# State space halves side by side, six shared PSUM banks, a re-measured issue planner and merged score sums in a two-layer hybrid model

## The chip, the cores and the metric

The kernel runs on one core of a Trainium2 chip. The metric is the device time of one launch in microseconds (us), the median of several runs. All engines of the core run their own instruction queues in order: TensorE (PE, with its weight loads, PEld), VectorE (DVE), ScalarE (ACT), GpSimd (POOL), and SyncE (SP), which issues DMAs.

## The reference

528 tokens (16 meta tokens and 512 others) of width 1024 pass two layers. Each layer mixes tokens in three ways at once, joins the three through one output projection, and then runs a gated feed-forward part:

```python
for l in range(2):
    hn = rmsnorm(h, norm1_g[l])
    sq, sk, sv, rq, rk, rv, rg, u = split(hn @ w_in[l])
    sb_o = stick_breaking(norm(sq), norm(sk), sv)        # 6 heads of 64: exp(logsig(z) + sums over later keys)
    ro = norm(retention(rotary(norm(rq)), rotary(norm(rk)), rv)) * silu(rg)   # 6 heads of 64
    so = s5_mixer(u, ...)          # 256 channels: complex diagonal recurrence, gelu, gate
    h = h + concat(sb_o, ro, so) @ w_out[l]
    hn = rmsnorm(h, norm2_g[l])
    h = h + (silu(hn @ w_gate[l]) * (hn @ w_up[l])) @ w_down[l]
```

The stick-breaking weight of a query and a key needs the sum of log(1 - sigmoid) over the later keys. The state space mixer (s5) needs, once per layer, matrices worked out from its small parameters.

## The kernel before, in words

Activations lie transposed, channels on the 128 partitions and tokens along the free axis: h is 8 tiles of 128 x 528. Every large product is made of three matmuls with 1-pass float32 parts, high x high, high x low and low x high, for each 128 x 128 weight block and each half of 264 tokens. `Unit` loads a block of weights into `wr`, ScalarE rounds it to `wh`, and VectorE or GpSimd subtracts for `wl`. `Norm.parts` makes `xh` (ScalarE) and `xl` (VectorE) of a chunk of h, `Norm.square` the squares, and `Norm.finish` the token scale R, with which VectorE multiplies every projection as it evacuates it. In the last layer the feed-forward part runs on 512 tokens, one matmul each.

One projection is 8 chunks x 3 x 2 = 48 matmuls into two PSUM banks named `pj`. Layer 1 has 22 of them in the order of `PROJ`; the first three are held (`HOLD`) until R is there. The mixers run beside the projections as Python generators ("lanes"): three stick-breaking pairs of heads (tiles z, e, sp, av), a retention lane (rtp, kv, sc, ro), a state space lane (`s5_mix`: es, fr, yps, ysm; `s5_glu`: the gate), the state space parameters (`s5_scalars`, `s5_params`: s5w, bb, btmp, gx, gg, ws, wps, bbd, kps, phasors phr, phi, py, st), and the norm of each head (hps). After each few matmuls `tick` lets lanes issue their next piece. A lane waits until the planner's clock reaches the estimated end of its last piece, which `Timed` and `mm` add up from costs written in the code:

```python
    V = Timed(nc.vector, "V", 70, 1.05)
    SC = Timed(nc.scalar, "SC", 180, 0.7)
    G = Timed(nc.gpsimd, "G", 110, 2.1)
...
        t = 2 * max(107.0, 2 * n) if rhs.dtype == F32 else max(107.0, n) + 3
```

PSUM has 8 banks. `free` lends four to stick-breaking scores and two to everything else a lane does; the projections take theirs, and the next projection's, outside this count. The tile framework places the instructions on the engines by the order of issue as priority, moving an instruction ahead where its inputs are there, and adds the waits; a tile's buffer is reused when its last reader is done.

In `sb_group`, the sums over later key tiles are matmuls with the all-ones matrix `ones`, one for each pair of a key tile and an earlier one in the same group, for the high and the low half of `sp`:

```python
        behind = [(j, q0, q1, o0, i) for j, q0, q1, o0 in g for i in place if i > j]
```

The parameters of layer 1 run on VectorE and GpSimd at the start (`engines` is (V, G)), those of layer 2 on GpSimd alone, (G, G), during layer 1's feed-forward part. One step of `outputs` is on VectorE in both: the imaginary half of `gg`. After the mixers, the output projection is added in three parts (`OUT_PARTS`), each when its inputs are ready: in layer 1 stick-breaking, state space, retention; in layer 2 state space, stick-breaking, retention.

Every instruction of a lane has the line of its helper in the profile: L122 is the `Timed` helper's call, L134 the matmul helper's, L140 the transpose's. So rows are told apart by tile names.

Of the kernel before, what the change touches and what calls it, by code (L numbers as in the profile page):

```python
# [8 lines left out]
F32 = mybir.dt.float32  # L9
# [22 lines left out]
BANKS = 2  # L32
# [57 lines left out]
def hybrid_kernel(ctx, tc, A, out, dbg=None):  # L90
# [16 lines left out]
    class Timed:  # L107


        def __init__(self, eng, key, fixed, each):  # L110
            self.eng, self.key, self.fixed, self.each = eng, key, fixed, each

        def __getattr__(self, name):
            f = getattr(self.eng, name)

            def issue(*a, **k):
                o = k.get("out", a[0] if a else None)
                n = 1
                for d in o.shape[1:]:
                    n *= d  # L120
                spend(self.key, self.fixed + self.each * n)
# [52 lines left out]
    def take(what, n):  # L174

        if free[what] < n:
            yield lambda: free[what] >= n
        free[what] -= n

    def banks(n):  # L180
        yield from take("bank", n)

    def freed(n, what="bank"):
        free[what] += n
# [350 lines left out]
    def s5_params(l, engines, scal, par):  # L535
# [74 lines left out]
        def outputs():  # L610
# [6 lines left out]
            for ri in range(2):  # L617
# [85 lines left out]
    def s5_mix(l, u, par, ys):  # L703
# [3 lines left out]
        for hf in range(2):  # L707
            ut = u[hf]
            uc = tt("uc")
            for t in range(4):  # L710
                for j in range(Q):
                    (SC.copy if (t + j) % 2 else V.tensor_copy)(
                        out=n3(uc)[32 * (3 - j):32 * (3 - j) + 32, t, :],
                        in_=ut[32 * t:32 * t + 32, :].rearrange("p (n q) -> p n q", q=Q)[:, :, j])
                yield
            pr, pi = ph[hf]
            fr, fi, y1, y2 = tt("fr"), tt("fi"), tt("y1"), tt("y2")
            for b in range(2):
                yield from banks(2)
# [567 lines left out]
```

## Time and profile before

| | |
|---|---|
| time, median of 3 runs (lowest to highest) | 1372.97 us (1372.7 to 1373.25) |
| time of the profiled execution | 1372.14 us |
| its span, first to last instruction | 1370.1 us |
| mean granted TensorE clock | 0.994 |
| matmul rows busy | 97% of the span |
| VectorE, ScalarE, GpSimd busy | 58%, 43%, 34% |

The span is what the trace covers; the time lies some 2 us above it. Ends of matmul rows are modelled, and rows overlap, so the starts of successive matmuls tell the pace, and the number of matmuls in a stretch tells how full it is. Where a row shows a bracket, it is the idle time of its engine just before it, and what ended it.

### The profile page before, as it was taken

Reading aid. Unit: us, or ns where it says so; the run is one execution under the profiler, and the core shown is the slowest. Engines: PE = TensorE matmul, PEld = TensorE weight load, DVE = VectorE, ACT = ScalarE, POOL = GpSimd, SP = SyncE. Lnnn points to the kernel's source line nnn. Section 1 sums busy time; section 2 is a strip of 40 time slices with the busy share of each in tenths; the row PEclk is TensorE's granted clock in tenths of the full one; section 3 lists DMA queues with packets and bytes.
Section 4 is the critical chain, followed back from the end, with each engine's and each line's share of the span. In section 5 each row is a group of like instructions: output and inputs, shape, how many; then the busy total and the mean of one; then the engine's idle time right before and its main releaser. Section 6 shows DMA issues by size and latency. Waiting matters only on the chain.

```text
span 1370.1 us, 22529 instructions
## 1 busy us (share of the span) xinstructions
PE 1335.6 (97%) x9188; PEld 1220.8 (89%) x9188; DVE 791.4 (58%) x1270; ACT 589.5 (43%) x936; POOL 464.9 (34%) x588
## 2 busy tenths in 40 slices
PE   6989999999899999999999999999999999999998
PEld 5988989989899999999999899998788888888886
DVE  8974657858456445533566874635485544554453
ACT  5447565446242223322355636664354422342231
POOL 5691545222799212200233451433222200220120
PEclk9999999999999999999999999999999999999999
DMA  4211222223221422232232221213232332333223
GB/s 157 70 62 47 84 66 87 78 69 98 95 79 48 123 78 93 93 93 93 78 93 93 71 94 47 92 43 102 62 123 93 92 95 90 99 102 93 92 81 104
DMA packets 38983, 118.26 MB, mean 86 GB/s; under 512 B 4960, under 2 KB 5472, under 8 KB 38880
## 3 DMA queue, kind: packets, MB, share of 16 engines
q1 hardware_dynamic: 38880, 116.82, 26.8%
q8 instruction: 72, 1.18, 0.4%
q14 instruction: 31, 0.25, 0.1%
HBM read 111.46 MB, written 2.10 MB: 83 GB/s over the span
## 4 chain that ended last, share of the span: by engine, by line
PE 82%; DVE 10%; POOL 3%; ACT 1%; issue 1%; DMA 1%; SPq 0%; DVEq 0%; ACTq 0%
PE pj L134 71%; PE z L134 5%; DVE ysm L122 2%; PE hps L134 1%; PE av L134 1%; PE ro L134 1%; DVE wl L122 1%; DVE s5w L122 1%; PE kps L134 1%; PE sc L134 1%; DVE gg L122 1%; DVE st L122 0%; DVE py L122 0%; POOL py L122 0%; DVE sp L122 0%
## 5 line engine op out<-in xcount | busy, mean ns | idle before, releaser
L134 PE MATMUL pj<-xh,wh 128*128 128x264 f32 (+1 forms) x1792 | 454.4, 311 | 16.8 <-ACT wh L122 5.1
L134 PE MATMUL pj<-xh,wl 128*128 128x264 f32 (+1 forms) x1792 | 453.3, 310 | 3.2 <-DVE wl L122 3.2
L134 PE MATMUL pj<-xl,wh 128*128 128x264 f32 (+1 forms) x1792 | 452.6, 310 | 2.6 <-DVE xl L122 2.6
L122 ACT CAST wh<-wr 128x1024 fp32r<-128x1024 f32 (+3 forms) x209 | 205.8, 987 | 418.8 <-PE pj L134 384.6
L134 PEld LDWEIGHTS pj<-xh,wh 128*128 128x128 f32 x1792 | 298.9, 190 | 36.0 <-issue 5.9
L134 PEld LDWEIGHTS pj<-xl,wh 128*128 128x128 f32 x1792 | 299.4, 190 | 20.5 <-DVE xl L122 3.3
L134 PEld LDWEIGHTS pj<-xh,wl 128*128 128x128 f32 x1792 | 298.9, 190 | 20.7 <-DVE wl L122 3.4
L122 DVE TENSOR_TENSOR wl<-wr,wh 128x1024 fp32r<-128x1024 f32 (+3 forms) x166 | 251.8, 1519 | 69.2 <-ACT wh L122 69.2
L134 PE MATMUL pj<-lo,wh 128*128 128x264 f32 (+1 forms) x720 | 193.4, 322 | 1.3 <-DVE lo L122 1.3
L134 PE MATMUL pj<-hi,wh 128*128 128x264 f32 (+1 forms) x720 | 193.2, 323 | 0.4 <-ACT hi L122 0.4
L134 PE MATMUL pj<-hi,wl 128*128 128x264 f32 (+1 forms) x720 | 193.1, 322 | 0.1
L122 POOL TENSOR_TENSOR up<-ga,up 128x528 f32<-128x528 f32 (+1 forms) x44 | 61.9, 1407 | 345.6 <-DVE up L122 345.5
L122 POOL TENSOR_TENSOR wl<-wr,wh 128x1024 fp32r<-128x1024 f32 (+2 forms) x43 | 96.2, 2237 | 159.4 <-ACT wh L122 153.6
L122 DVE TENSOR_TENSOR h<-h,pj 128x264 f32<-128x264 f32 (+1 forms) x144 | 69.1, 510 | 140.4 <-PE pj L134 140.0
L134 PEld LDWEIGHTS pj<-hi,wh 128*128 128x128 f32 x720 | 120.3, 189 | 11.9 <-ACT hi L122 0.7
L134 PEld LDWEIGHTS pj<-lo,wh 128*128 128x128 f32 x720 | 120.0, 188 | 12.1 <-DVE lo L122 1.5
L134 PEld LDWEIGHTS pj<-hi,wl 128*128 128x128 f32 x720 | 120.0, 189 | 11.1 <-DVE wl L122 0.5
L122 POOL TENSOR_TENSOR lo<-ga,hi 128x528 fp32r<-128x528 f32 (+1 forms) x44 | 58.5, 1330 | 158.0 <-ACT hi L122 157.9
L122 DVE TENSOR_TENSOR up<-pj,R 128x264 f32<-128x264 f32 (+1 forms) x66 | 32.1, 514 | 94.2 <-PE pj L134 94.2
L122 DVE TENSOR_TENSOR ga<-si,up 128x528 f32<-128x528 f32 (+1 forms) x44 | 31.7, 720 | 72.7 <-ACT si L122 57.2
L122 ACT ACTIVATE si<-si,bias 128x528 f32<-128x528 f32 (+1 forms) x44 | 32.2, 731 | 93.9 <-DVE si L122 93.9
L122 POOL TENSOR_TENSOR lo<-sp,hi 128x432 fp32r<-128x432 f32 (+2 forms) x36 | 44.4, 1245 | 73.3 <-ACT hi L122 71.7
(221 smaller groups left out, 1533.9 us busy)
## 6 DMA issues: line engine op xcount, KB each, us to landing
wr<-in_w_in_dram SPq DMA_DIRECT2D x45, 512.0 KB, 3.5
wr<-in_w_gate_dram SPq DMA_DIRECT2D x44, 512.0 KB, 3.5
wr<-in_w_up_dram SPq DMA_DIRECT2D x44, 512.0 KB, 3.5
wr<-in_w_down_dram SPq DMA_DIRECT2D x32, 512.0 KB, 3.6
wr<-in_w_out_dram SPq DMA_DIRECT2D x16, 384.0 KB, 3.3
wr<-in_w_down_dram SPq DMA_DIRECT2D x16, 384.0 KB, 3.1
rc<-in_rope_dram SPq DMA_DIRECT2D x12, 264.0 KB, 3.8
rs<-in_rope_dram SPq DMA_DIRECT2D x12, 264.0 KB, 4.0
```

Of the source, the lines that this page charges most:

```text
L122: return f(*a, **k)
L134: nc.tensor.matmul(out, lhsT=lhsT, rhs=rhs, start=start, stop=stop, skip_group_check=more)
```

## The change

It does the following.

- The start loads the first two weight blocks in pieces between the chunks of h, splits them there, and takes the squares one chunk behind. The first two projections run chunk by chunk together (`two_proj`), the third after them. The state space parameters are spawned after `nrm.finish()`, not before the projections.
- `s5_mix` handles one half of the channels, and the lane spawns it twice, the first when the first half of u is there.
- `BANKS` goes from 2 to 6, and the scores take from the same six (at most four).
- `Timed` gets costs for each kind of operation; strided outputs count twice. The matmul's cost changes too.
- In `sb_group` the matmuls with `ones` that read the same operand for two query tiles become one, with an output of two pieces and an operand read twice.
- In `outputs` the sign of the imaginary half goes into `bbd` and into `xi`; the `gg` step becomes an addition on the parameters' engine. The lane then waits 2 us longer, by the planner's clock, before the `kps` matmuls.

```diff
-BANKS = 2
+BANKS = 6
...
-    V = Timed(nc.vector, "V", 70, 1.05)
-    SC = Timed(nc.scalar, "SC", 180, 0.7)
-    G = Timed(nc.gpsimd, "G", 110, 2.1)
+    V = Timed(nc.vector, "V", {"one": (150, 1.05), "two": (160, 1.2), "tensor_scalar": (150, 0.55),
+                               "tensor_tensor_scan": (180, 2.2)})
+    SC = Timed(nc.scalar, "SC", {"one": (230, 0.8), "two": (230, 0.8)})
+    G = Timed(nc.gpsimd, "G", {"one": (180, 2.1), "two": (180, 2.1), "memset": (100, 0.85)})
...
-        n = out.shape[-1] / 2.4
-        t = 2 * max(107.0, 2 * n) if rhs.dtype == F32 else max(107.0, n) + 3
+        n = math.prod(out.shape[1:]) / 2.4
+        t = 2 * max(109.0, 2 * n + 3) if rhs.dtype == F32 else max(110.0, 1.055 * n + 5)
...
-                        if ri:
-                            V.scalar_tensor_tensor(out=o, in0=a, scalar=-1.0, in1=b, op0=ALU.mult, op1=ALU.subtract)
-                        else:
-                            sub(o, a, b)
+                        (add if ri else sub)(o, a, b)
...
-                    engines[ri].tensor_copy(
+                    engines[ri].tensor_scalar(
...
-                        in_=src[64 * q:64 * q + 64])
+                        in0=src[64 * q:64 * q + 64], scalar1=-1.0 if ri else 1.0, scalar2=None, op0=ALU.mult)
+            now[0][1] += 2000
...
-            V.tensor_tensor(out=xi, in0=fr, in1=pi, op=ALU.mult)
+        V.scalar_tensor_tensor(out=xi, in0=fr, scalar=-1.0, in1=pi, op0=ALU.mult, op1=ALU.mult)
...
+        behind = {}
+        for j, q0, q1, o0 in g:
+            for i, (g1, o1, p0) in place.items():
+                if i > j:
+                    a = max(q0, p0)
+                    behind.setdefault(i, (g1, o1 + a - p0, q1 - a, []))[3].append(o0 + a - q0)
...
+        for g1, o1, w, to in behind.values():
+            d, c = zp[:, to[0]:to[0] + w], slice(o1, o1 + w)
+            if len(to) == 2:
+                f = to[1] - to[0]
+                d = zp[:, to[0] + w - f:to[0] + w + f].rearrange("p (t c) -> p t c", t=2)[:, :, f - w:]
             for part in range(2):
-                mm(zp[:, o0 + a - q0:o0 + q1 - q0], lhsT=ones, rhs=hl[g1][part][:, o1 + a - p0:o1 + q1 - p0],
+                x = hl[g1][part][:, c]
+                mm(d, lhsT=ones, rhs=x[:, None, :].to_broadcast([P, 2, w]) if len(to) == 2 else x,
                    start=False, stop=True, more=True)
...
-        freed(1, "scores")
+        freed(1, "scores", "bank")
...
-                yield from take("scores", 2)
+                yield from take(2, "scores", "bank")
...
+    units += [Unit(*plan[0]), Unit(*plan[1])]
+    for k in range(KD):
         nc.sync.dma_start(out=h[k], in_=A["h0"][k])
...
+        if k < 4:
+            q = [(units[k % 2], k // 2, 4)]
+        elif k < 6:
+            q = [(units[k % 2], 1, 2)]
+        for u, i, pieces in q:
+            c = u.load(i, pieces)
+            nrm.parts(k)
+            for _ in u.split(c):
+                pass
...
+        if k:
+            nrm.square(k - 1)
+    nrm.square(KD - 1)
...
-    spawn(first_params())
...
+        def two_proj():
+
+            ws = [weight(), weight()]
+            pss = [open_ps(T), open_ps(T)]
+            xh, xl = nrm.x
+            for k in range(KD):
+                for ps, w in zip(pss, ws):
+                    mm3(ps, tuple(t[:, k:k + 1, :] for t in w), (xh[k:k + 1], xl[k:k + 1]), first=k == 0, last=k == KD - 1)
+            return pss
...
-            yield lambda: ("u", 1) in got and bool(par)
-            ys, so = [], []
-            yield from s5_mix(l, [got["u", 0], got["u", 1]], par[0], ys)
-            yield from s5_glu(l, ys, so)
+            yield lambda: ("u", 0) in got and bool(par)
+            ys, so = {}, []
+            spawn(s5_mix(l, 0, got["u", 0], par[0], ys), now[0][1])
+            yield lambda: ("u", 1) in got
+            spawn(s5_mix(l, 1, got["u", 1], par[0], ys), now[0][1])
+            yield lambda: len(ys) == 2
+            yield from s5_glu(l, [ys[0], ys[1]], so)
...
             if i == HOLD[l]:
                 nrm.finish()
+                if l == 0:
+                    spawn(first_params())
```

## Rows read from the trace of the kernel before

**Rows 1.** The page's first part: busy time, share of the span, instructions.

```profile
PE 1335.6 (97%) x9188; PEld 1220.8 (89%) x9188; DVE 791.4 (58%) x1270; ACT 589.5 (43%) x936; POOL 464.9 (34%) x588
```

**Rows 2.** Stretches: length, then busy us (instructions) of PE, PEld, DVE, ACT, POOL; clock.

```profile
0.00:13.00 13.00, 5.76 (x23) 5.15 (x24) 7.45 (x27) 7.93 (x14) 8.36 (x36) 1.00 0.80 262
13.00:25.00 12.00, 9.43 (x75) 9.00 (x75) 11.93 (x26) 7.87 (x13) 9.52 (x5) 1.00 0.23 78
25.00:37.40 12.40, 8.39 (x55) 7.96 (x53) 11.55 (x47) 3.15 (x5) 3.97 (x6) 0.86 0.25 89
74.00:92.00 18.00, 13.48 (x83) 12.82 (x82) 16.92 (x55) 10.18 (x19) 15.85 (x40) 0.81 0.09 30
279.00:287.00 8.00, 6.30 (x37) 5.63 (x36) 4.95 (x14) 3.26 (x9) 0.59 (x2) 0.79 0.17 49
366.00:375.50 9.50, 5.72 (x36) 5.54 (x35) 6.91 (x10) 2.15 (x3) 9.42 (x14) 0.82 0.13 45
500.00:525.00 25.00, 25.00 (x208) 25.00 (x207) 14.13 (x18) 9.39 (x13) 5.34 (x4) 1.00 0.26 86
```

**Rows 3.** Timeline of TensorE, front: start us, length us, what [idle before <-ended by].

```profile
28.95 0.52 PE L134 MATMUL pj<-xh,wl 128*128 128x264 f32 x2 [3.19 <-DVE wl L122]
...
35.93 0.28 PE L134 MATMUL nps<-hi,meanw 128*128 128x264 f32 x1
...
37.42 0.39 PE L134 MATMUL pj<-xh,wh 128*128 128x264 f32 x1 [0.83 <-ACT R L122]
```

**Rows 4.** Timelines of ScalarE, VectorE and GpSimd, front.

```profile
12.62 1.99 ACT L122 ACTIVATE xh<-h,cols 128x528 fp32r<-128x528 f32 x3
...
12.93 2.38 DVE L122 TENSOR_SCALAR s5w<-s5w 128x16 f32<-128x16 f32 x2
...
19.61 0.76 DVE L122 SCALAR_TENSOR_TENSOR xl<-h,cols,xh 128x528 fp32r<-128x528 f32 x1
...
12.80 2.41 POOL L122 TENSOR_TENSOR wl<-wr,wh 128x1024 fp32r<-128x1024 f32 x1 [1.90 <-ACT wh L122]
```

**Rows 5.** Timeline of TensorE, sums over later key tiles.

```profile
159.85 0.23 PE L134 MATMUL z<-hi,ones 128*128 128x144 f32 x1
...
160.02 0.22 PE L134 MATMUL z<-hi,ones 128*128 128x16 f32 x1
...
160.21 0.36 PE L134 MATMUL z<-hi,ones 128*128 128x256 f32 x1
```

**Rows 6.** Groups of TensorE by shape: count | busy us, mean ns | idle.

```profile
L134 PE MATMUL z<-lo,ones 128*128 128x16 f32 x72 | 17.8, 258 | 0.0
```

**Rows 7.** Timelines of TensorE and VectorE, 77 to 88 us.

```profile
77.44 0.39 PE L134 MATMUL pj<-xh,wh 128*128 128x264 f32 x1 [2.52 <-ACT we L122]
...
87.83 0.39 PE L134 MATMUL pj<-xh,wh 128*128 128x264 f32 x1 [1.16 <-DVE sq L122]
...
79.58 2.34 DVE L122 TENSOR_TENSOR st<-st 128x4 f32<-128x4 f32 x1
```

**Rows 8.** Stretches of tile es alone (PE, PEld, DVE), and TensorE's timeline at 282.

```profile
140.00:170.00 30.00, 2.12 (x16) 2.03 (x16) 2.87 (x8) 1.00 0.30 91
...
200.00:230.00 30.00, 2.13 (x16) 1.97 (x16) 2.86 (x8) 1.00 0.22 68
...
281.96 0.51 PE L134 MATMUL pj<-lo,wh 128*128 128x264 f32 x2 [1.26 <-DVE lo L122]
```

**Rows 9.** Timelines of GpSimd, VectorE and TensorE, 365 to 372 us.

```profile
365.40 2.64 POOL L122 TENSOR_TENSOR gx<-braw,s5p 128x640 f32<-128x640 f32 x2
...
368.07 2.94 DVE L122 SCALAR_TENSOR_TENSOR gg<-gx,gx 64x320 f32<-64x320 f32 x4 [3.96 <-POOL gx L122]
...
371.61 0.56 PE L134 MATMUL pj<-xh,wh 128*128 128x264 f32 x1 [3.78 <-DVE ga L122]
```

**Rows 10.** Waits of TensorE, whole span: us in total, times, longest us.

```profile
PE kps L134 <- POOL bbd L122: 1.5, 1, 1.5
...
PE hps L134 <- ACT hsq L122: 1.3, 1, 1.3
```

More of the change, by code (lines that the diff above doesn't have):

```diff
@@ L107, in hybrid_kernel, with __init__ @@
     class Timed:
-        def __init__(self, eng, key, fixed, each):
-            self.eng, self.key, self.fixed, self.each = eng, key, fixed, each
+        def __init__(self, eng, key, kinds):
+            self.eng, self.key, self.kinds = eng, key, kinds
         def __getattr__(self, name):
@@ L117, in issue @@
                 o = k.get("out", a[0] if a else None)
[L118 to L121, printed above, removed]
+                n = math.prod(o.shape[1:]) * (2 if o.ap[-1][0] > 1 else 1)
+                two = [x for x in (k.get("in0"), k.get("in1")) if x is not None]
+                kind = name if name in self.kinds else "two" if len(two) == 2 and not any(
+                    x.space == PSUM for x in two) else "one"
+                fixed, each = self.kinds[kind]
+                spend(self.key, fixed + each * n)
                 return f(*a, **k)
             return issue
-    V = Timed(nc.vector, "V", 70, 1.05)
-    SC = Timed(nc.scalar, "SC", 180, 0.7)
-    G = Timed(nc.gpsimd, "G", 110, 2.1)
+    V = Timed(nc.vector, "V", {"one": (150, 1.05), "two": (160, 1.2), "tensor_scalar": (150, 0.55),
+                               "tensor_tensor_scan": (180, 2.2)})
+    SC = Timed(nc.scalar, "SC", {"one": (230, 0.8), "two": (230, 0.8)})
+    G = Timed(nc.gpsimd, "G", {"one": (180, 2.1), "two": (180, 2.1), "memset": (100, 0.85)})
     def mm(out, lhsT, rhs, start, stop, more=False):
-        n = out.shape[-1] / 2.4
-        t = 2 * max(107.0, 2 * n) if rhs.dtype == F32 else max(107.0, n) + 3
+        n = math.prod(out.shape[1:]) / 2.4
+        t = 2 * max(109.0, 2 * n + 3) if rhs.dtype == F32 else max(110.0, 1.055 * n + 5)
         spend("PE", t / 2 if 64 in (rhs.shape[0], out.shape[0]) else t)
@@ L172, in hybrid_kernel, with take, freed @@
     free = {"bank": BANKS, "scores": ZBANKS, "group": GROUPS}
[L174 to L178, printed above, removed]
+    def take(n, *what):
+        if any(free[w] < n for w in what):
+            yield lambda: all(free[w] >= n for w in what)
+        for w in what:
+            free[w] -= n
     def banks(n):
-        yield from take("bank", n)
-    def freed(n, what="bank"):
-        free[what] += n
+        yield from take(n, "bank")
+    def freed(n, *what):
+        for w in what or ("bank",):
+            free[w] += n
     def tick(most=TICKS):
@@ L791, in s5_glu @@
+        ys[hf] = y
+        yield
     def s5_glu(l, ys, res):
@@ L881, in sb_pair @@
         sets = ((G_A,), (G_B2, G_B1))
-        yield from take("group", 2)
+        yield from take(2, "group")
         started.append(weights(sets[0]))
@@ L887, in sb_pair @@
             if groups is sets[0]:
-                yield from take("group", 4)
+                yield from take(4, "group")
                 started.append(weights(sets[1]))
@@ L1075, in hybrid_kernel, with proj @@
         mix = [None] * 8
-        def proj(n, p):
-            w = weight()
+        def proj(w):
             ps = open_ps(T)
@@ L1129, in hybrid_kernel @@
         for i, (n, p) in enumerate(proj_order(l)):
-            held.append((n, p, proj(n, p)))
+            if l == 0 and i < 2:
+                if i == 0:
+                    first = two_proj()
+                held.append((n, p, first[i]))
+            else:
+                held.append((n, p, proj(weight())))
             if i == HOLD[l]:
                 nrm.finish()
+                if l == 0:
+                    spawn(first_params())
             if i >= HOLD[l]:
```

191 lines of the change are left out of this document (85 added, 106 removed).

## The prediction

> **What bounds the kernel now.** I read the page's busy times first. The matmul rows cover 97% of the span [rows 1], so time can come off only where TensorE has less to do or stands still; a faster VectorE, ScalarE or GpSimd is worth something only through TensorE. But a busy row is no proof of full speed, so next I cut the span into stretches and counted matmuls. In an undisturbed stretch of the feed-forward part 208 matmuls of 264 columns pass in 25 us, 0.120 us each, at granted clock 1.00, the 2.4 GHz level [rows 2]. Against that yardstick five places stand out.
>
> - Front: 23, 75 and 55 matmuls by 13, 25 and 37.4 us, 153 in all, 18.4 us of work in 37.4 us [rows 2]. 19 us are lost.
> - 74 to 92: 83 where 150 would fit, 8.0 us lost, clock 0.81 [rows 2].
> - 279 to 287: 37 where 67 would fit, 3.6 us, clock 0.79 [rows 2].
> - 366 to 375.5: 36 where 79 would fit, 5.2 us, clock 0.82 [rows 2].
> - Single waits elsewhere, of which two of 1.5 and 1.3 us are shown [rows 10].
>
> A clock below 1.00 is a piece of such a stretch at 1.2 GHz: TensorE had just stood still (3.78 us before 371.61 [rows 9]), and then runs at half speed. So a wait that goes takes a second bill with it, which the counts contain.
>
> Last I read, with the timeline of each engine, what ends these waits. I sum against the profiled execution's own 1372.14 us (span 1370.1); it lies 0.83 us under the median of the runs, 0.06%, and I use one number for both.
>
> **Part 1: the first two blocks side by side (front).** Before, the first projection takes 6 matmuls from each chunk of the hidden state as it arrives, and the second and third follow. After, two weight blocks come in with the chunks and each chunk feeds 12. The DMAs move the same bytes; one more issue stands in SP's queue. When is the last chunk ready? ScalarE has its high half at 14.61 (12.62 + 1.99), but VectorE finishes the low half only at 20.37 [rows 4]: it is in order, and two 16-column scalar operations of the state space part, put in while it was free, took 2.38 us beside GpSimd's 2.41 us subtraction [rows 4]. After, ScalarE carries squares and smaller weight pieces between the chunks, and the scalars are spawned only after the norm's end. They have no input but a small table, so some may still slip in. I take 18.5 for the last low half, between 15.4 (14.61 + one 0.76 operation) and 20.4. By then at least 23 + 5.5 / 0.120 = 69 of the 96 matmuls are done (23 if no more run before 13 us than now), at most the 84 of seven chunks; I take 79. Left are 17 and 48 of the third projection, 65 x 0.120 = 7.8, and the norm's end, 35.93 to 37.42 = 1.5 [rows 3]: 27.8 instead of 37.4. **Gain 10** (9.6). Bounds: 12 if the low half comes at 16.5 (25.8); 3 if it comes at 20.4 with seven chunks done (60 x 0.120 + 1.5 later, 29.1) and the wait of 3.19 us for a weight's low half [rows 3] comes back behind the moved scalars with its half clock, 1.7 (0.14 of 12.4 [rows 2]): 33.9.
>
> **Part 2: issue order by measured durations.** The planner's clock ran ahead of the chip: it took 113 ns for a 264-column matmul that takes 120 [rows 2], and 70 ns as VectorE's fixed cost. So pieces of side work are issued sooner than VectorE can do them, and they clump. From 74 to 92 VectorE is busy 16.92 of 18 us [rows 2], largely with tiny phasor steps, one of which takes 2.34 [rows 7]; the softplus and the evacuations that TensorE needs queue behind, and it waits 2.52 and 1.16 [rows 7]. With costs near the measured ones these steps are spaced. They can go later without harm: the mixer first uses the parameters after 140 [rows 8]. But VectorE's work is not reduced. Of the 8.0 lost I take **4** (0 if the clump only moves, 8 if it dissolves). The single waits go the same way, and the product of the parameters gets 2 us more before its matmuls: of the 1.5 and 1.3 [rows 10] **1.5** (0 to 2.8).
>
> **Part 3: merged sums.** The sums over later key tiles, matmuls with the all-ones matrix, are issued once for two query tiles where the operand is the same. Counted from the code: for each head, pair and layer (12) the high and low halves go from 13 to 8 each, 312 to 192 in all. Of every two 16-wide ones one goes; the trace has 72 of the low half [rows 6], so 36 pairs of halves go. A pair starts 0.19 us before its successor (160.02 to 160.21) [rows 5]: 36 x 0.19 = 6.8. Of the 144-wide 12 pairs go, at 0.17 (159.85 to 160.02) [rows 5], but the merged 288 columns should cost 288/264 of 0.120 = 0.13 each, 0.26 a pair, for 0.34: 12 x 0.08 = 1.0. For the 256-wide, whose merged output has no gap and twice the columns, I take nothing. Sum **8**. TensorE is saturated around these rows, so nothing hides it. Not shown is a matmul whose output lies in two pieces with a gap: 96 of the merged ones write so (the 16s and 144s), and all read the same operand twice. Upper bound 8 (no extra cost); lower 0 (a merged one costs as much as two). I take 8, since in the rows the cost follows the columns above a floor.
>
> No row here shows a gapped write. The Trainium skill's page "PSUM — Partial Sum Buffer" (Specifications) says that any non-contiguous access pattern slows matmuls significantly, without a figure; by it the lower end holds and the whole sum comes to 1352 instead of 1344.
>
> **Part 4: the state space halves side by side.** Now the second half's first products run 60 us after the first's (both 16 matmuls, in 140 to 170 and 200 to 230 [rows 8]), and the gate of this branch ends so late that the output projection over it waits 1.26 us for its low half at 281.96 [rows 8], at the place of the 3.6. Overlapped halves end tens of us earlier. **3** (0 to 3.6). What is late next is the third retention pair, which also needs TensorE there.
>
> **Part 5: the sign moved in the output matrices.** In layer 2's parameters, VectorE's four gg operations wait 3.96 us for GpSimd's gx; the evacuation ga stands behind them in the same queue, and TensorE waits 3.78 for it [rows 9]. The change makes them plain additions on the parameters' engine, here GpSimd, so VectorE no longer waits. GpSimd, busy 9.42 of 9.5 us there [rows 2], gets four operations, each below the 1.3 of a gx [rows 9], up to 5.3 us, behind which the feed-forward's up products wait, and VectorE's last product behind those. **4.5** of 5.2 (0 if that wait takes its place). xi as a three-operand form, and the bbd scaling, stay beside TensorE's work: nothing; without that cover some 0.3 us each.
>
> **Part 6: six shared banks.** Side work may hold six banks at any time, not two plus four for scores. This lets retention and headnorm go on sooner; I count it in the parts above. Against it stand waits of the projections, which take two banks outside the count: the wait at 77.44 is one of a projection for ScalarE's copy out of a wps bank [rows 7]. I charge **3** for new waits of this kind and of the new order (0 to 20).
>
> **Sum.** 10 + 4 + 1.5 + 8 + 3 + 4.5 - 3 = 28: 1372.14 - 28 = **1344 us**.
>
> **Rivals.**
> *Gapped writes cost (0.13).* The merged sums bring nothing: 28 - 8 = 20, 1352. It decides from 81 ns more for each of the 96 (7.8 / 96). For: no such row. Against: only the smooth rows.
> *VectorE takes the front back (0.16).* It is busy 11.93 of 12, 11.55 of 12.4 and 16.92 of 18 us in the stretches from 13 on [rows 2]. If TensorE comes 10 us earlier to evacuations that are no earlier, it waits there. Parts 1 and 2's first term (14) go: 1358. Against: the scalars, phasors and parameters can lie behind.
> *Projections wait for banks (0.08): slower.* With six banks lent out, the next projection needs the two that the last one filled, and waits for VectorE. Some 41 projections run beside side work (22 + 22 - 3). At 28 / 41 = 0.68 us each the gain is gone; at the 1.16 of [rows 7] each it is 48 against 31, 1389. Against: before, 2 + 4 could be lent too, and only waits like 77.44 came of it.
>
> **How the numbers follow.** The forecast has 0.63. All terms at their best give 39.6, 1332, and a little more of the front's 19 makes 1329. Front at 3, gapped writes at full cost, the others at half (2 + 1.4 + 1.5 + 2.2) give some 10 to 12, with rival 2 in view: 1360. Below I leave 0.08, above 0.12. A change within 0.2% (2.7 us) is about what cannot be told from none. Faster 0.91, same 0.02 (where rivals 2 and 3 meet), slower 0.07.
>
> **What would show it.** The fourth projection starts near 28, not 37.4. Ones matmuls number 192, and the 16-wide step from one to the next stays near 0.1 us. The wait of 3.78 for ga and that of 1.26 for the gate's low half are gone; 74 to 92 (now earlier) holds more matmuls at a clock nearer 1.00. The prediction is wrong if the merged rows are spaced twice as far, if projections wait for copies out of other lanes' banks, or if the front's 10 us are lost again before 100.

## The result, and the profile after

The changed kernel takes 1380.97 us, the median of 4 runs (1379.42 to 1382.28); the kernel before took 1373.1 in the same comparison. The ratio is 1.0059, 95% interval 1.0047 to 1.0071: **slower by 0.6%**, where 2% faster was forecast. The profiled execution took 1382.3 us (span 1380.6, mean granted clock 0.986 against 0.994).

The page's busy times answer to [rows 1]; 120 matmuls fewer are recorded, and TensorE's busy time is the same.

```profile
PE 1335.9 (97%) x9068; PEld 1216.3 (88%) x9068; DVE 784.2 (57%) x1261; ACT 587.9 (43%) x937; POOL 470.2 (34%) x598
```

Stretches of the changed kernel, columns as in [rows 2].

```profile
0.00:13.00 13.00, 7.43 (x41) 6.85 (x42) 8.26 (x26) 9.24 (x18) 11.14 (x38) 1.00 0.78 251
13.00:25.00 12.00, 9.27 (x72) 8.63 (x71) 11.57 (x29) 6.23 (x10) 5.62 (x5) 1.00 0.30 107
74.00:92.00 18.00, 13.95 (x92) 13.00 (x94) 17.83 (x79) 5.79 (x12) 15.24 (x44) 0.91 0.17 60
175.00:200.00 25.00, 22.59 (x156) 18.84 (x155) 22.64 (x39) 10.97 (x23) 12.45 (x10) 0.93 0.16 53
279.00:287.00 8.00, 8.00 (x68) 8.00 (x67) 7.28 (x15) 3.62 (x6) 3.95 (x4) 1.00 0.18 51
296.00:306.00 10.00, 8.55 (x40) 7.14 (x41) 1.06 (x3) 4.70 (x9) 1.17 (x1) 0.51 0.08 30
375.00:400.00 25.00, 15.76 (x106) 15.14 (x106) 8.50 (x14) 9.09 (x14) 24.64 (x61) 0.73 0.11 35
500.00:525.00 25.00, 25.00 (x208) 25.00 (x207) 13.26 (x18) 9.48 (x13) 4.19 (x4) 1.00 0.25 86
```

Three of these stretches in the kernel before:

```profile
175.00:200.00 25.00, 24.11 (x194) 22.49 (x190) 15.37 (x37) 15.45 (x32) 9.05 (x6) 1.00 0.20 65
296.00:306.00 10.00, 10.00 (x87) 9.70 (x84) 5.55 (x12) 5.88 (x10) 3.18 (x2) 1.00 0.29 80
375.00:400.00 25.00, 25.00 (x209) 25.00 (x209) 13.36 (x22) 13.52 (x20) 21.54 (x47) 1.00 0.26 85
```

The places that the prediction aimed at are better: 41 matmuls by 13 us instead of 23, 92 instead of 83 from 74 to 92, 68 instead of 37 from 279 to 287 at full clock. But three stretches that were full are not any more: 194 to 156, 87 to 40, 209 to 106 matmuls. At 0.120 us each (an estimate, since not all matmuls are alike) that is some 4.6 + 5.6 + 12.4 = 22.6 us, with TensorE at 1.2 GHz in part of each. The waits behind them (view of waits, TensorE, the largest of 41.0 us in all; 30.8 before):

```profile
PE wps L144 <- POOL ws L125: 9.2, 2, 8.2
PE pj L138 <- ACT wh L125: 5.5, 1, 5.5
PE hps L138 <- ACT hsq L125: 3.6, 3, 1.3
PE pj L138 <- DVE u L125: 3.3, 1, 3.3
PE vps L144 <- DVE sv L125: 2.9, 2, 2.2
PE ro L138 <- DVE sc L125: 2.6, 3, 1.3
PE pj L138 <- DVE wl L125: 2.5, 1, 2.5
PE z L138 <- DVE rk L125: 2.4, 1, 2.4
```

The 3.78 for ga [rows 9] and the 1.26 for the gate's low half [rows 8] are not in the list; wps on ws, over five times as long as either of [rows 10], is new.

By stages, in the profiled executions: layer 1's mixing part (to the first matmul of its feed-forward part) takes 322.8 us instead of 320.6, its feed-forward part (to layer 2's first projection) 405.8 instead of 398.6, and all that follows 1.0 more. So 7.2 of the 10.5 us that the span is longer lie in the feed-forward part that holds the stretch from 375 to 400.

**From 175 to 200 it is VectorE.** Its timeline, then TensorE's row at 182.91:

```profile
169.91 1.78 DVE L125 TENSOR_TENSOR_SCAN fr<-rho,fr 128x132 f32<-128x132 f32 x2
...
176.40 3.39 DVE L125 TENSOR_TENSOR_SCAN fi<-rho,fi 128x132 f32<-128x132 f32 x2
...
181.78 0.75 DVE L125 TENSOR_TENSOR_SCAN fi<-rho,fi 128x132 f32<-128x132 f32 x2
182.45 0.75 DVE L125 TENSOR_TENSOR rk<-pj,R 128x264 f32<-128x264 f32 x2
```

```profile
182.91 0.34 PE L138 MATMUL z<-maskA,identb 128*128 128x432 bf16 x1 [2.41 <-DVE rk L125]
```

The scans of both halves of the state space lane stand in one run, with the evacuation of rk behind them. A scores' matmul waits 2.41 us for it; rk is no operand of it, so I read it as the PSUM bank that the evacuation frees. The clock record has TensorE at 1.2 GHz from 183.5 to 186.9.

**From 375 to 400 it is GpSimd.** Its timeline, and TensorE's:

```profile
367.69 2.85 POOL L125 TENSOR_TENSOR gx<-braw,s5p 128x640 f32<-128x640 f32 x2
...
370.91 4.46 POOL L125 TENSOR_TENSOR gg<-gx,gx 64x320 f32<-64x320 f32 x4
...
377.47 2.73 POOL L125 TENSOR_TENSOR btmp<-bb,s5p 128x512 f32<-128x512 f32 x2
...
380.30 1.29 POOL L125 TENSOR_TENSOR up<-ga,up 128x528 f32<-128x528 f32 x1
381.55 6.38 POOL L125 TENSOR_TENSOR ws<-btmp,btmp 64x256 f32<-64x256 f32 x8
```

```profile
384.27 1.97 PE L144 MATMUL wps<-ident,ws 128*128 128x128 f32 x8 [8.18 <-POOL ws L125]
```

The four gg additions that came from VectorE take 4.46 us of a queue in which the ws products of the same parameters stand later. TensorE has come to the transposes of ws, and it is in order: 8.18 us, and 1.2 GHz from 378.0 to 391.7.

**From 296 to 306** the last retention pair is alone (ro behind sc, hps behind hsq for 1.35 us at 302.45), 10.2 us at 1.2 GHz.

### The profile page after: what moved, and what is told of

The parts are those of the page before. It is cut to its first block, busy times and chain, and to the rows that moved or that the text cites. A ratio compares the mean times of both kernels' runs of the same rounds, so it can differ in the third digit from the quotient of the medians.

```text
span 1380.6 us, 22305 instructions
## 1 busy us (share of the span) xinstructions
PE 1335.9 (97%) x9068; PEld 1216.3 (88%) x9068; DVE 784.2 (57%) x1261; ACT 587.9 (43%) x937; POOL 470.2 (34%) x598
## 4 chain that ended last, share of the span: by engine, by line
PE 79%; DVE 11%; POOL 5%; ACT 2%; issue 1%; DMA 1%; SPq 0%; DVEq 0%; POOLq 0%
PE pj L138 68%; PE z L138 4%; PE hps L138 2%; PE av L138 1%; PE ro L138 1%; DVE fr L125 1%; DVE wl L125 1%; DVE ysm L125 1%; DVE fi L125 1%; DVE y L125 1%; DVE s5w L125 1%; POOL py L125 1%; POOL st L125 1%; POOL gg L125 1%; PE kps L138 1%
## 5 line engine op out<-in xcount | busy, mean ns | idle before, releaser
L138 PE MATMUL pj<-xh,wh 128*128 128x264 f32 (+1 forms) x1792 | 446.3, 309 | 9.1 <-ACT wh L125 5.5
L138 PE MATMUL pj<-xh,wl 128*128 128x264 f32 (+1 forms) x1792 | 446.8, 309 | 2.5 <-DVE wl L125 2.5
L138 PE MATMUL pj<-xl,wh 128*128 128x264 f32 (+1 forms) x1792 | 447.0, 310 | 0.3 <-DVE xl L125 0.2
L138 PEld LDWEIGHTS pj<-xh,wh 128*128 128x128 f32 x1792 | 295.7, 190 | 26.4 <-ACT wh L125 5.5
L138 PEld LDWEIGHTS pj<-xl,wh 128*128 128x128 f32 x1792 | 296.3, 190 | 18.1 <-DVE xl L125 0.9
L125 DVE TENSOR_TENSOR wl<-wr,wh 128x1024 fp32r<-128x1024 f32 (+3 forms) x165 | 246.7, 1495 | 76.3 <-ACT wh L125 76.2
L125 POOL TENSOR_TENSOR wl<-wr,wh 128x1024 fp32r<-128x1024 f32 (+3 forms) x45 | 97.3, 2162 | 151.8 <-ACT wh L125 132.9
L138 PEld LDWEIGHTS pj<-hi,wl 128*128 128x128 f32 x720 | 120.4, 189 | 11.1 <-DVE wl L125 0.5
```

The costliest lines, as they stand in the source:

```text
L138: nc.tensor.matmul(out, lhsT=lhsT, rhs=rhs, start=start, stop=stop, skip_group_check=more)
```

## The experiments

For every profiled kernel the time is split in three. *Waits* is the idle time ahead of TensorE's instructions, summed. *Half speed* is half of the time at 1.2 GHz in which TensorE was busy. *Rest* is the profiled execution's time less both. "Sums" says whether the all-ones sums are merged.

| kernel | median us | ratio to before, 95% | sums | profiled | waits | half speed | rest |
|---|---|---|---|---|---|---|---|
| before | 1373 | | no | 1372.1 | 30.8 | 8.4 | 1332.9 |
| changed | 1380.97 | 1.0047 to 1.0071 | yes | 1382.3 | 41.0 | 14.4 | 1326.8 |
| e1 sums alone | 1376.71 | 1.0018 to 1.0043 | yes | 1376.4 | 41.4 | 14.6 | 1320.4 |
| e7 start alone | 1387.62 | 1.0092 to 1.0123 | no | 1388.0 | 44.0 | 14.6 | 1329.4 |
| e2 sign back | 1381.64 | 1.0044 to 1.0074 | yes | 1381.1 | 39.4 | 14.3 | 1327.4 |
| e3 halves in turn | 1380.45 | 1.0039 to 1.0073 | yes | 1379.7 | 40.9 | 14.4 | 1324.4 |
| e4 costs back | 1388.93 | 1.0100 to 1.0133 | yes | 1392.1 | 44.6 | 21.6 | 1325.9 |
| e5 banks back | 1395.64 | 1.0144 to 1.0174 | yes | 1396.1 | 54.7 | 21.0 | 1320.4 |
| e6 start back | 1387.52 | 1.0096 to 1.0126 | yes | 1388.1 | 47.1 | 17.2 | 1323.7 |
| e8 products later | 1380.30 | 1.0034 to 1.0072 | yes | 1377.1 | 37.2 | 9.8 | 1330.0 |
| e9 second after scans | 1374.57 | 0.9999 to 1.0019 | yes | | | | |
| e10 layer 2 in turn | 1367.83 | 0.9948 to 0.9974 | yes | 1367.4 | 29.3 | 11.1 | 1327.0 |
| e11 scans, then turn | **1361.87** | 0.9908 to 0.9938 | yes | 1364.6 | 31.8 | 8.1 | 1324.8 |
| e12 e11, sums back | 1376.92 | 1.0015 to 1.0046 | no | 1376.8 | 33.3 | 8.4 | 1335.2 |
| e13 e11, old start | 1380.39 | 1.0034 to 1.0070 | yes | 1378.0 | 43.1 | 13.8 | 1321.1 |
| e14 before, 230 ns | 1394.69 | 1.0141 to 1.0171 | no | 1393.5 | 43.9 | 14.7 | 1335.0 |
| e15 changed, 230 ns | 1373.36 | 0.9995 to 1.0013 | yes | 1374.9 | 40.2 | 11.1 | 1323.6 |
| e16 before, 170 ns | 1381.14 | 1.0046 to 1.0076 | no | 1381.5 | 34.8 | 14.4 | 1332.2 |
| e17 changed, 170 ns | 1381.90 | 1.0049 to 1.0082 | yes | 1381.9 | 44.7 | 11.6 | 1325.6 |
| e18 e11, 230 ns | 1365.44 | 0.9931 to 0.9960 | yes | 1364.9 | 34.4 | 10.0 | 1320.5 |

The rest has a mean of 1332.9 us over the 5 profiled kernels without merged sums (1329.4 to 1335.2) and 1324.4 over the 14 with them (1320.4 to 1330.0). What differs beside that is waits and half speed: 39.2 us together before, 55.4 changed, 39.9 in e11.

### One part undone, one part alone

e2 takes the sign back into VectorE's gg step; bbd and xi are as before, too, and the lane's 2 us are gone. The first hunk:

```diff
-                        (add if ri else sub)(o, a, b)
+                        if ri:
+                            V.scalar_tensor_tensor(out=o, in0=a, scalar=-1.0, in1=b, op0=ALU.mult, op1=ALU.subtract)
+                        else:
+                            sub(o, a, b)
...
```

> The changed kernel with the old sign handling alone: the imaginary gg step is again a VectorE three-operand operation, bbd a copy, no 2 us delay. Theory (the four additions on GpSimd lengthen its queue in layer 1's feed-forward part, and the transposes of ws that TensorE has in its order wait for it): the wait of 8.2 us for ws and its 13.7 us of half clock go, the old wait of 3.8 us for ga comes back; 12 lost there becomes 5.5, so about 1374. Rival (the wait for ws comes of the new costs or the six banks, which put the transposes earlier in TensorE's order): the wait for ws stays within 2 us of 8, and the time stays at 1379 to 1382, or grows if both waits add.

The wait for ws falls from 9.2 to 2.0 in all, that for ga returns with 3.8, and layer 1's feed-forward part passes its first 864 matmuls in 119.0 us, 118.6 before and 125.3 changed (starts in TensorE's timeline). Those 6 us are real in their place. The other stages are longer in this profile, layer 1's mixing part by 0.9, layer 2's by 1.6 and the last feed-forward part by 1.8 us, and the median does not move: the theory has its mechanism and misses its 1374.

e3 runs the halves one after the other, e4 takes back the old cost lines, e5 the old bank counts:

```diff
-            spawn(s5_mix(l, 0, got["u", 0], par[0], ys), now[0][1])
             yield lambda: ("u", 1) in got
-            spawn(s5_mix(l, 1, got["u", 1], par[0], ys), now[0][1])
-            yield lambda: len(ys) == 2
+            for hf in range(2):
+                yield from s5_mix(l, hf, got["u", hf], par[0], ys)
```

```diff
-    V = Timed(nc.vector, "V", {"one": (150, 1.05), "two": (160, 1.2), "tensor_scalar": (150, 0.55),
-                               "tensor_tensor_scan": (180, 2.2)})
+    V = Timed(nc.vector, "V", 70, 1.05)
...
-        t = 2 * max(109.0, 2 * n + 3) if rhs.dtype == F32 else max(110.0, 1.055 * n + 5)
+        t = 2 * max(107.0, 2 * n) if rhs.dtype == F32 else max(107.0, n) + 3
```

```diff
-BANKS = 6
+BANKS = 2
...
-        freed(1, "scores", "bank")
+        freed(1, "scores")
...
-                yield from take(2, "scores", "bank")
+                yield from take(2, "scores")
```

> The changed kernel with the two state space halves one after the other again, nothing else. Theory (two halves at once jam VectorE at 150 to 200 us, 22.6 of 25 us busy, and everything TensorE needs of it comes late): the waits at 173 to 187 go and the retention lane's second pair starts near 235, not 251; 6 to 10 us faster, 1371 to 1375; the wait for the gate's low half near 280 may return with 1 to 5. Rival (retention is late because of banks or because of the costs): second pair still at 250, time within 3 us of 1381 or slower.

> The changed kernel with the old planner costs for the four engines, nothing else. Theory (the longer costs space the pieces of the retention lane, which is the last to end in both layers): third retention pair starts earlier, 275 to 280 and not 286, and the time falls by 3 to 8 us to 1373 to 1378, though the clump of phasor steps at 74 to 92 may come back with up to 4. Rival (the costs are right and what delays is the jam on VectorE or the banks): time equal or slower, 1381 to 1390.

> The changed kernel with two banks for lanes and four for scores again, nothing else. Theory (six shared banks let scores and state space hold what the retention lane needs, and let more side work start than VectorE can serve): retention's second pair starts near 235, TensorE's waits at 165 to 190 shrink; 4 to 10 us faster. Rival (six banks help or do nothing): within 3 us, or slower by up to 10 because lanes wait for two banks again.

e3: in layer 1 the second retention pair (its first rtp) starts at 219.8 us instead of 251.4, as the theory has it, and the first output projection comes at 239.5 instead of 249.4. But now the state space lane is the last, and TensorE stands for it at the end of the mixing part. The stretch from 275 to 300 of e3:

```profile
275.00:300.00 25.00, 15.72 (x84) 14.22 (x84) 9.72 (x19) 12.27 (x22) 1.30 (x1) 0.66 0.00 1
```

In layer 2 the mixing part takes 276.3 us instead of 281.5. The sum is no change. e4 and e5 are 8 and 15 us slower than the changed kernel, where both theories had them faster; e4 lies in its rival's range, e5 above both. The third retention pair of e4 starts at 285.6 us (286.5 in the changed kernel) and the second of e5 at 256.3 (251.4), so neither comes earlier as its theory has it. These runs give no sign that the costs or the six banks made the kernel slow; each is one order of issue, and the control below shows how far one such order can be from the next. In e4 the wait for ws has shrunk as well, to 4.5 us in all with 2.4 the longest, and layer 1's feed-forward part takes 400.3 us: by this run the 8.18 us need the new costs beside the new sign. In e5 kv waits 11.5 us for kt, with 20.5 us at 1.2 GHz from 260 on.

e1 is the kernel before with the merged sums alone, e7 with the new start alone (whole hunks of the change, here their first lines); e6 is the changed kernel with the start's hunk undone.

```diff
-        behind = [(j, q0, q1, o0, i) for j, q0, q1, o0 in g for i in place if i > j]
+        behind = {}
...
```

```diff
+    units += [Unit(*plan[0]), Unit(*plan[1])]
+    for k in range(KD):
...
-    spawn(first_params())
...
```

> The kernel before with the merged all-ones sums alone. In the changed kernel's trace the merged matmuls are 192 and take 25 us of TensorE instead of 33, so 8 us of work are gone. Theory A (the gain of the sums is real and is only covered up by new waits elsewhere): 1373 - 8 = about 1365, 1363 to 1368. Theory B (the mixing part ends when its last lane ends, so work taken from TensorE before that point only turns into waiting): 1372 to 1374, and the waits of TensorE grow by what the sums lost. Theory C (a gapped write costs something that the starts do not show): above 1374.

> The kernel before with the new start alone. Theory A (7 us reach the end): about 1366, 1364 to 1368. Theory B (lost again by the first output projection, which starts at 252.4 before): 1372 to 1374, first output projection within 2 us of 252.4 though the fourth projection is near 30. Theory C (later parameters delay the state space lane): above 1375.

> The changed kernel with the old start (one projection per chunk, parameters spawned at once) and all else as changed. In the changed kernel the fourth projection starts at 30.5 instead of 37.4. Theory A (the front's 7 us reach the end): 1381 + 7 = 1388, with the fourth projection near 37. Theory B (what the front gains is lost again before the output projection, because the lanes end no sooner): 1380 to 1382. Theory C (the late parameters and the scalar operations that moved behind the front cost more than it brings): below 1379.

e1 does less work (rest 1320.4) and is slower: theory A's work with theory B's waits, 10.6 us more of them and 6.2 of half speed. Its time lies in theory C's range, but for the reason that C gives no row speaks. One thing beside the sums differs: the old cost line counts the last axis alone, so the planner of e1 takes a merged matmul for half as wide. The first output projection comes at 241.3 us instead of 252.4, and the gain is lost behind it. Its stretches at the end of layer 1's mixing part, and its largest wait, one for the operand of the output projection:

```profile
250.00:275.00 25.00, 21.09 (x163) 19.71 (x161) 21.94 (x51) 7.29 (x15) 8.49 (x9) 0.86 0.29 75
275.00:300.00 25.00, 16.15 (x109) 14.92 (x110) 11.50 (x28) 12.27 (x24) 3.08 (x3) 0.79 0.04 8
```

```profile
PE pj L134 <- ACT hi L122: 7.1, 1, 7.1
```

e7 has the fourth projection at 32.3 us and the first output projection at 245.4 instead of 252.4, so the front's 7 us came that far. It loses all of it and more at the same end:

```profile
275.00:300.00 25.00, 13.93 (x85) 11.98 (x84) 11.38 (x25) 11.82 (x26) 3.44 (x3) 0.66 0.06 17
```

```profile
PE kv L134 <- ACT kt L122: 9.5, 1, 9.5
```

The kernel before has 209 and 174 matmuls in these two stretches. e6 is near theory A by its time (+6.6), but its eighth projection starts at 75.3 us instead of 66.2: more than the front.

### The named places, one by one

e8 delays the transposes of layer 2's parameters; no work goes:

```diff
+            if l:
+                now[0][1] += 8000
             yield
             for hf in range(2):
                 yield from banks(1)
                 ps = bank("wps")
```

> The changed kernel, where in the parameters of layer 2 alone the lane waits 8 us longer, by the planner's clock, before the transposes of ws are issued; no work is taken out. In the changed kernel TensorE stands 8.2 us at 384.3 on these transposes, because GpSimd's gg additions and btmp products lie ahead of ws in its queue, and is at half clock from 378.0 to 391.7. Theory A (the wait is one of placement: TensorE is in order and took the transposes before GpSimd was done): the wait is gone, the half-clock stretch too, the stretch 375 to 400 holds some 200 matmuls instead of 106, and the time falls by 9 to 12 us to 1369 to 1372. Theory B (what GpSimd does there is late for other things too, the up products first): the wait goes to the up products or the split and the time falls by less than 4, 1377 to 1381.

The place behaves as theory A says. The stretch from 375 to 400 of e8, and its wait:

```profile
375.00:400.00 25.00, 21.89 (x168) 21.50 (x167) 13.80 (x21) 11.17 (x17) 24.71 (x59) 0.93 0.17 56
```

```profile
PE wps L144 <- POOL ws L125: 2.4, 1, 2.4
```

62 more matmuls. The first 864 of the feed-forward part take 118.3 us again, the whole part 400.6 instead of 405.8. The median (of 1377.1 to 1382.4) hardly moves: as a time, theory B's range. Nor are the 5 us by which the profiled execution is faster the edit's alone. Up to 370 us the four engines of both kernels run the same instructions in the same order, and yet layer 1's mixing part took 317.5 us here and 322.8 in the changed kernel; layer 2's took 284.1 instead of 281.5, and the last feed-forward part 2.8 more. Which wait the longer executions have isn't recorded.

e9 and e11 let the second half start after the first half's scans, e9 in both layers, e11 in layer 1 alone; e10 and e11 run layer 2 in turn. All keep e8's delay. e11's lines, of which the first stands behind the scans in `s5_mix`:

```diff
+        scanned.add((l, hf))
...
-            yield lambda: ("u", 1) in got
+            yield lambda: ("u", 1) in got and ((l, 0) in scanned if l == 0 else 0 in ys)
```

> The changed kernel with the later products of the run before, and the second half of the state space lane started only when the first half's scans are issued, in both layers. With the products later alone the profiled time was 1377.1. In the changed kernel VectorE has both halves' scans in one run from 168 to 184 us, the evacuation of rk stands behind them, TensorE waits 2.4 us and is at half clock to 186.9: against smooth spacing 9.7 us are lost in 175 to 200, 3.3 before. Theory A (the two halves side by side jam VectorE): the loss in 175 to 200 falls by 5 to 7 and the profiled time is 1370 to 1373. Theory B (the time is set by the lane that ends last, whichever it is): the 175 to 200 loss falls too, but as much comes back from 250 to 310, 1376 to 1380.

> The changed kernel with the later products, and the state space halves one after the other in layer 2 alone. Layer 2's mixing part took 279.4 us before, 281.5 in the changed kernel, and 276.3 where the halves ran in turn in both layers. Theory A (in layer 2, where the state space branch is the first input of the output projection, the halves side by side cost 5 us on VectorE): the mixing part of layer 2 near 277 and the profiled time 1370 to 1373. Theory B (that 276.3 came from the timing at which layer 2 began, and the order does nothing): 281 to 284, 1376 to 1379.

> Both: the second half after the first's scans in layer 1, in turn in layer 2, products later. If both theories A hold, 1377 - 6 - 5 = 1366, 1364 to 1368, faster than the kernel before. If only one holds, 1370 to 1373. If the lane that ends last sets the time in both layers, 1376 to 1380.

e9: 1374.57, 5.7 under e8, between the two ranges. Its profile is of one execution of 7387 us that isn't compared. e10: the mixing part of layer 2 takes 274.2 us (e8: 284.1), and the time is under theory A's range. Stretches of e8, then of e10, in layer 2:

```profile
750.00:775.00 25.00, 23.95 (x195) 22.41 (x195) 24.79 (x41) 10.73 (x21) 11.62 (x9) 1.00 0.18 62
775.00:800.00 25.00, 22.88 (x161) 21.08 (x160) 17.99 (x39) 17.05 (x32) 8.98 (x6) 0.93 0.21 65
```

```profile
750.00:775.00 25.00, 25.00 (x207) 23.87 (x206) 17.96 (x33) 14.67 (x27) 10.06 (x6) 1.00 0.25 86
775.00:800.00 25.00, 25.00 (x195) 23.57 (x194) 18.24 (x27) 17.14 (x33) 13.05 (x8) 1.00 0.34 108
```

With the halves side by side VectorE is full (24.79 of 25 us) and TensorE is not; in turn it is the other way round. e11 does the same in layer 1, at that place:

```profile
175.00:200.00 25.00, 25.00 (x212) 23.50 (x211) 11.85 (x25) 15.74 (x32) 11.24 (x7) 1.00 0.28 92
```

212 matmuls instead of e8's 159, and 1361.87 us: 0.8% faster than the kernel before, the fastest of the study and under all of its ranges. In its profile, though, the gain of layer 1 does not reach the end of the mixing part. A later stretch, and a wait that e8 does not have:

```profile
275.00:300.00 25.00, 20.02 (x152) 18.23 (x153) 14.60 (x35) 12.39 (x24) 6.10 (x8) 0.86 0.12 32
```

```profile
PE kv L138 <- ACT kt L125: 5.2, 1, 5.2
```

e8 has 191 matmuls there. The mixing part takes 318.1 us in e11, 317.5 in e8 and 320.9 in e10, and e8 and e10 have the same order up to layer 2. So where the 6.0 us between the medians of e10 and e11 come from isn't shown. Layer 2's part is firmer. Over the profiled kernels with merged sums its mixing part takes 271.3 to 276.3 us where the halves run in turn (6 kernels) and 275.8 to 290.1 where they run side by side (8).

### Sums and start on the better kernel

> The mended kernel of the run before (1361.9) with the all-ones sums not merged. Theory A (a merged pair of matmuls is work saved, and where no lane ends late it reaches the end): 1361.9 + 8 to 10 = 1370 to 1372. Theory B (the mixing part's lanes set its end, TensorE's work there is worth nothing): 1360 to 1364. Theory C (any such step re-rolls the order of issue by more than its own worth): anything from 1362 to 1380, with waits at places that have no all-ones sums near.

> The mended kernel (1361.9) with the old start. Theory A (the front's 5 to 7 us reach the end): 1367 to 1369. Theory B (they are lost before the first output projection): 1361 to 1363. Theory C (new order of issue): outside both, up to 1375.

The edits are the hunks of e1 and e7, undone on e11, which the expectations call the mended kernel. Without the merged sums the profiled time rises by 12.3 us: 10.4 in the rest, 1.5 in waits, 0.3 in half speed. That is theory A's mechanism. The median rises by 15.1, which is outside A's range and inside C's; its executions lie between 1372.9 and 1383.0. The old start costs 13.4 in the profiled time although the fourth projection is only 3.9 us later (36.4 against 32.5): 11.3 are waits, 8.0 of them from 40 to 330 us, and 5.7 half speed; the rest falls by 3.7. That is theory C's mechanism; the median, 1380.39, lies above its bound of 1375 even.

### The control: 30 ns in one constant

`LEAD` says how far ahead of the planner's clock a lane's next piece may be issued. It touches no work and no dependency.

```diff
-LEAD = 200
+LEAD = 230
```

> A control: the kernel before with the constant by which a lane's next piece may be issued ahead of the planner's clock at 230 ns instead of 200, nothing else. If the order of issue is a matter of chance of several us: 1366 to 1390. If it is not: 1372 to 1374.

> The same control on the changed kernel: 230 ns instead of 200. If the order of issue is a matter of chance of several us: anything from 1368 to 1392. If it is not: 1380 to 1382.

> The control on the kernel before with 170 ns (200 gives 1373, 230 gave 1394.7). If 200 is a good draw of a wide spread: 1380 to 1395. If 230 was the odd one: 1371 to 1376.

> The control on the changed kernel with 170 ns (200 gave 1381.0, 230 gave 1373.4). If its draws lie about 1377 with a spread of some 5: 1371 to 1384. If 230 was a good one among worse: above 1384.

> The control on the mended kernel with 230 ns (200 gave 1361.9). If the mended places are what brings the time: 1358 to 1368. If 1361.9 was one good draw: 1370 to 1380, with new waits at other places.

At 170, 200 and 230 ns the kernel before takes 1381.1, 1373.0 and 1394.7; the changed one 1381.9, 1381.0 and 1373.4; e11 at 200 and 230 takes 1361.9 and 1365.4. So a constant without work moves the kernel before by up to 22 us, nearly three times the result, and e14 lies even outside the range given for chance. The changed kernel moves by 0.9 and -7.6. In e14 the loss is at the same place as in e1 and e7:

```profile
275.00:300.00 25.00, 16.58 (x100) 14.62 (x101) 13.93 (x30) 13.99 (x27) 2.41 (x2) 0.70 0.07 21
```

```profile
PE kv L134 <- ACT kt L122: 6.3, 1, 6.3
```

At 200 the kernel before has the fewest waits of the 5 without merged sums. Against its own neighbours the change is even (170) or 21 us faster (230). Both draws of e11 lie under all six of the other two kernels.

Not everything is redrawn. Layer 1's feed-forward part takes 404.9 to 406.5 us in all six profiled kernels that have the new sign handling with the new costs and without e8's delay (changed, e3, e5, e6, e15, e17), and 398.4 to 400.8 in the thirteen others. In these six the longest wait for ws is 8.2 us. So this loss of some 6 us is the change's own in every order drawn, and not luck. What moves with the order is the mixing parts: layer 1's takes 320.6, 326.2 and 338.9 us in the three draws of the kernel before.

## Why the prediction was wrong

The step that failed is part 6, "I charge 3 for new waits of this kind and of the new order (0 to 20)". In the profiled runs the waits that are new or longer add up to 28.6 us and those that are gone or shorter to 18.7; in all, waits rise by 10.2 us and half speed by 6.0. Of the 38.1 us between the forecast and the profiled time, 36.2 are waits and half speed (20 less were forecast, if all parts but the sums are counted there, and 16.2 more came) and 1.9 the rest (8 less were forecast, 6.1 came). Beside it failed what the sum took for granted: that all other waits stay where they were. No part of this change leaves the order of issue alone, and the control shows what a new order costs with no part at all: 8 to 22 us on the kernel before, 0.9 more to 7.6 less on the changed one. One of the new waits is no matter of the order: the 8.2 us for ws, of part 5, come in every order drawn. The low waits of the kernel before were the best of three draws, which is luck, and the prediction read them as a base from which gains are taken off. The forecast's low chance for slower, 0.07, rested on the wait for the projections' banks as the only mechanism.

- **Part 1 (10, front).** The fourth projection starts at 30.48, not 27.8: 6.9. VectorE and TensorE of the changed kernel:

```profile
20.64 0.77 DVE L125 SCALAR_TENSOR_TENSOR xl<-h,cols,xh 128x528 fp32r<-128x528 f32 x1
```

```profile
17.32 0.51 PE L138 MATMUL pj<-xh,wl 128*128 128x264 f32 x2 [2.46 <-DVE wl L125]
...
30.48 0.39 PE L138 MATMUL pj<-xh,wh 128*128 128x264 f32 x1 [0.33 <-ACT R L125]
```

  The last low half is ready at 21.41, later than the 18.5 that I took and than the bound of 20.4. By then 81 matmuls had started, within the bounds of 69 and 84. The remaining 15 and 48 by 0.120, and 1.5, give 30.5: the sum is right, the time put into it was not. The premise behind it failed. The scalar operations were to lie behind the norm's end, but the trace has 31 of them, 8.8 us, on VectorE before the last low half (23 and 9.5 us in the kernel before, up to the same time). One of 1.33 us stands ahead of the `wl` of a piece, 1.79 from 15.47, for which TensorE waits 2.46. Whether those 6.9 reach the end can't be told: alone the start goes with +15, undone with +7 and +19, all within what the control moves.
- **Part 2 (5.5, order).** 74 to 92 gains 9 matmuls, 1.1 us, in a stretch that now lies differently; VectorE is busier, 17.83 of 18. Mis-sized. The old costs are 8 slower in e4, again within the control.
- **Part 3 (8, sums).** Right in mechanism and size: 192 matmuls, and 8.5 us less rest over 19 profiled kernels. A stretch of the changed kernel, to be held against [rows 5]:

```profile
176.22 0.39 PE L138 MATMUL z<-hi,ones 128*128 128x512 f32 x1
176.44 0.40 PE L138 MATMUL z<-lo,ones 128*128 128x512 f32 x1
176.68 0.29 PE L138 MATMUL z<-hi,ones 128*128 128x288 f32 x1
176.81 0.29 PE L138 MATMUL z<-lo,ones 128*128 128x288 f32 x1
176.94 0.18 PE L138 MATMUL z<-hi,ones 128*128 128x32 f32 x1
176.97 0.26 PE L138 MATMUL z<-lo,ones 128*128 128x32 f32 x1
177.08 0.36 PE L138 MATMUL z<-hi,ones 128*128 128x256 f32 x1
```

  The merged pair with a gapped output of 2 x 16 columns takes 0.14 us to its successor here, a pair of single 16 took 0.19 in [rows 5]; in the medians both take 0.18 to 0.19 a pair; the gapped 288 take 0.13 each, as estimated. The rival of gapped writes is out. The rule of the Trainium skill's page "PSUM — Partial Sum Buffer" (Specifications), that a non-contiguous pattern slows matmuls significantly, is not borne out for these two shapes.
- **Part 4 (3, halves).** The wait at 282 is gone as said. The step that failed is the cover: I looked at where the lane ends and not at VectorE where it runs. Two halves at once fill VectorE, and the evacuation behind their scans stops TensorE. Undone in layer 2 and put off in layer 1 the medians fall by 12.5 and 6.0 us (e8 to e10 to e11); in the profiles layer 2's mixing part is 9.9 us shorter from e8 to e10, and for the second they show no place. The "third retention pair" was rightly named as late next; it stands alone from 296 to 306.
- **Part 5 (4.5, sign).** The wait for ga went. I named GpSimd's longer queue as what could take its place, but looked for the up products behind it; it was the transposes of ws, 8.18 us with 13.7 us at 1.2 GHz. Price in 375 to 400: 103 matmuls, 12.4 us, against the 5.2 that were to be won. Over the whole feed-forward part the loss is 7.2, and it stands in every order drawn. e2 and e8 show both sides of it.
- **Rivals.** VectorE takes the front back: at the front only in part (the 2.46 us), but it is VectorE that fills at 175 and at 750. Projections wait for banks: one wait is of that kind, 3.3 us for the evacuation of u, in place of the 2.52 of [rows 7]; the larger ones are for operands, and with two banks e5 is not better.

Two smaller errors: a layer has 23 projections, not the 22 of the text, and so 43 beside side work (23 + 23 - 3); only the third rival's price hangs on it. And the range reached up to 1360, though the bound of 20 for part 6 alone led to 1361, with the other terms at their middle.

What stays open: why the order at 200 ns has so few waits in the kernel before, and how 30 ns becomes a wait of 6 us for kt; that chain was not followed. Three draws of each kernel don't give the change's mean effect. That e11 gains by its structure is shown for layer 2's mixing part and for layer 1's feed-forward part, not for layer 1's mixing part, and its time rests on two draws.

## What to carry to other kernels

Where lanes of side work are put between matmuls by a planner, a change has two effects: the work that it takes away, which adds up as forecast (8.5 us here), and a new order of issue, which re-rolls the waits (8 to 22 us here). Before a single-part result is read as the part's worth, move a planner constant that does no work, on both kernels, and see how far the time goes. Then compare stages over all the orders drawn: what holds in every one (some 6 us in layer 1's feed-forward part here) is the part's own. Then mend places, not parts: find the stretch with fewer matmuls than its neighbours, the full queue of another engine in it, and the one evacuation or transpose that stands behind.

## What the runs showed of the hardware

- A stop costs more than its length, and unevenly: after 2.41 us of waiting the clock record has 3.4 us at 1.2 GHz, around the 8.18 us wait 13.7, in e5 from 260 on 20.5. Over the profiled runs half speed takes 8 to 22 us beside 29 to 55 of waits.
- A 16-column float32 matmul and one of 2 x 16 gapped columns start their successors alike, in 0.11 us for the low halves and 0.07 for the high ones (medians of 72 and 36).
- The same instructions in the same order do not take the same time: layer 1's mixing part took 317.5, 320.9 and 322.8 us in the profiled executions of e8, e10 and the changed kernel.
- One execution of e9 took 7387 us, with 31 matmuls in a 25 us stretch instead of 208 and a recorded clock of 1.00; its other nine lie between 1372.6 and 1374.9. The cause is not known.
